# Rotary embedding over 134 MB: two of each partition's sixteen rows of batch 0 stored early by SyncE, and the cosine and sine tables requested from the ScalarE queue

## The chip, the cores and the metric

The kernel runs on one core of a Trainium2 chip. The metric is the device time of one execution in microseconds, lower is better. Each timing is the median of 3 to 11 executions. A profile's "span" is the stretch from the first to the last instruction of the program. The device time is somewhat longer than the span.

## The reference

```python
# x: 8 x 2048 x 16 x 64 float32;  cos, sin: 2048 x 32 float32
x1, x2 = x[..., :32], x[..., 32:]
out1 = x1 * cos - x2 * sin          # cos, sin broadcast over batch and heads
out2 = x1 * sin + x2 * cos
out  = concatenate([out1, out2], axis=-1)      # float32
```

One batch is 8.39 MB in float32. Eight are read and eight are written; the arithmetic is six operations per output pair.

## The kernel before

A row position `s` is split as `s = p*16 + j`, so that each of the 128 partitions holds 16 neighbouring rows. "Two rows" below means two of the 16 in every partition, 1.05 MB in f32. All compute is in f16. The DMAs issued from GpSimd convert f32 to f16 on loading and back on storing; they stand in one ring, in order. Two rows of batch 0 come separately as f32 (`head`) by SyncE, so that something moves before the ring starts, and the last two rows of batch 7 leave the same way.

```python
    J = S // P; NBUF = 5; JA = 2                        # J = 16
    head = const_pool.tile([P, JA, H, D], f32)
    nc.sync.dma_start(out=head..., in_=x0[:, 0:JA, :]...)
    nc.sync.dma_start(out=sin_f, in_=sin.rearrange("(p j) d -> p j d", j=J))
    nc.sync.dma_start(out=cos_f, in_=cos.rearrange("(p j) d -> p j d", j=J))
    # load(b): GpSimd DMA, f32 -> f16 (rows 2..15 for batch 0); store(b, xt): GpSimd DMA, f16 -> f32

    def rotate(xt):
        v = tmp_pool.tile([P, J, H, D], f16)
        # ... broadcasts of sin, -sin and cos over the heads (cut)
        nc.vector.tensor_mul(out=v[:, :, :, 0:Dh], in0=xt[:, :, :, Dh:D], in1=neg_b)
        nc.vector.tensor_mul(out=v[:, :, :, Dh:D], in0=xt[:, :, :, 0:Dh], in1=sin_b)
        nc.vector.tensor_mul(out=xw, in0=xw, in1=cos_b)
        nc.vector.tensor_add(out=xa, in0=xa, in1=v...)

    tiles = [load(b) for b in range(NBUF)]              # five loads at once
    # ScalarE: head -> tile 0, sin_f -> sin_h, -sin_f -> neg_h, cos_f -> cos_h   (cut)
    for b in range(B):
        rotate(tiles[b])
        if b < B - 1:
            store(b, tiles[b])
        if b + NBUF < B:
            tiles.append(load(b + NBUF))                # waits until a buffer's store has landed
    # batch 7 goes out in three parts: 9 rows, 5 rows (ring), 2 rows (ScalarE cast to head, SyncE)   (cut)
```

Of the kernel before, what the change touches and what calls it, by code (L numbers as in the profile page):

```python
# [1 line left out]

# [4 lines left out]


@with_exitstack  # L10
def kernel(
    ctx: ExitStack,
    tc: tile.TileContext,
    x: bass.AP,
    cos: bass.AP,
    sin: bass.AP,
    out: bass.AP,
):
    nc = tc.nc
    f16 = mybir.dt.float16  # L20
    f32 = mybir.dt.float32

    B, S, H, D = x.shape
    Dh = D // 2
    P = nc.NUM_PARTITIONS
    J = S // P
    NBUF = 5

    const_pool = ctx.enter_context(tc.tile_pool(name="rope_const", bufs=1))
    io_pool = ctx.enter_context(tc.tile_pool(name="rope_io", bufs=NBUF))  # L30
    tmp_pool = ctx.enter_context(tc.tile_pool(name="rope_tmp", bufs=1))

    JA = 2
    head = const_pool.tile([P, JA, H, D], f32)
    x0 = x[0].rearrange("(p j) h d -> p j (h d)", j=J)
    nc.sync.dma_start(  # L36
        out=head.rearrange("p j h d -> p (j h d)"),
        in_=x0[:, 0:JA, :].rearrange("p j f -> p (j f)"),
    )
    sin_f = const_pool.tile([P, J, Dh], f32)  # L40
    cos_f = const_pool.tile([P, J, Dh], f32)
    cos_h = const_pool.tile([P, J, Dh], f16)
    sin_h = const_pool.tile([P, J, Dh], f16)
    neg_h = const_pool.tile([P, J, Dh], f16)
    nc.sync.dma_start(out=sin_f, in_=sin.rearrange("(p j) d -> p j d", j=J))  # L45
    nc.sync.dma_start(out=cos_f, in_=cos.rearrange("(p j) d -> p j d", j=J))

    def load(b):
        xt = io_pool.tile([P, J, H, D], f16)
        j0 = JA if b == 0 else 0  # L50
        nc.gpsimd.dma_start(  # L51
            out=xt[:, j0:J, :, :].rearrange("p j h d -> p (j h d)"),
            in_=x[b].rearrange("(p j) h d -> p j (h d)", j=J)[:, j0:J, :].rearrange("p j f -> p (j f)"),
        )
        return xt

    def store(b, xt):
        nc.gpsimd.dma_start(  # L58
            out=out[b].rearrange("(p j) h d -> p (j h d)", j=J), in_=xt
        )  # L60

    def rotate(xt):
        v = tmp_pool.tile([P, J, H, D], f16)
        sin_b = sin_h.unsqueeze(2).to_broadcast([P, J, H, Dh])
        neg_b = neg_h.unsqueeze(2).to_broadcast([P, J, H, Dh])
        cos_b = cos_h.unsqueeze(2).to_broadcast([P, J, 2 * H, Dh])
        nc.vector.tensor_mul(out=v[:, :, :, 0:Dh], in0=xt[:, :, :, Dh:D], in1=neg_b)  # L67
        nc.vector.tensor_mul(out=v[:, :, :, Dh:D], in0=xt[:, :, :, 0:Dh], in1=sin_b)  # L68
        xw = xt.rearrange("p j h (e d) -> p j (h e) d", d=Dh)
        nc.vector.tensor_mul(out=xw, in0=xw, in1=cos_b)  # L70
        xa = xt.rearrange("p j h d -> p (j h d)")
        nc.vector.tensor_add(out=xa, in0=xa, in1=v.rearrange("p j h d -> p (j h d)"))  # L72

    tiles = [load(b) for b in range(NBUF)]
    nc.scalar.copy(  # L75
        out=tiles[0][:, 0:JA, :, :].rearrange("p j h d -> p (j h d)"),
        in_=head.rearrange("p j h d -> p (j h d)"),
    )
    nc.scalar.copy(out=sin_h, in_=sin_f)  # L79
    nc.scalar.mul(out=neg_h, in_=sin_f, mul=-1.0)  # L80
    nc.scalar.copy(out=cos_h, in_=cos_f)  # L81
    def part(b, j0, j1):
        return (
            out[b].rearrange("(p j) h d -> p j (h d)", j=J)[:, j0:j1, :].rearrange("p j f -> p (j f)"),
            tiles[b][:, j0:j1, :, :].rearrange("p j h d -> p (j h d)"),
        )

    for b in range(B):
        rotate(tiles[b])
        if b < B - 1:  # L90
            store(b, tiles[b])
        if b + NBUF < B:
            tiles.append(load(b + NBUF))
    dst, src = part(B - 1, 0, 9)
    gate = nc.gpsimd.dma_start(out=dst, in_=src)  # L95
    dst, src = part(B - 1, 9, J - JA)
    rest = nc.gpsimd.dma_start(out=dst, in_=src)  # L97
    tc.add_manual_dep(
        rest.ins,
        gate.ins.name,  # L100
        mybir.DependencyInfo(mybir.DependencyClass.NoSync, mybir.DependencyReason.DATA),
        reason="order of the ring",
    )
    dst, src = part(B - 1, J - JA, J)
    nc.scalar.copy(out=head.rearrange("p j h d -> p (j h d)"), in_=src)  # L105
    end = nc.sync.dma_start(out=dst, in_=head.rearrange("p j h d -> p (j h d)"))
    tc.add_manual_dep(
        end.ins,
        gate.ins.name,
        mybir.DependencyInfo(mybir.DependencyClass.Sync, mybir.DependencyReason.DATA),  # L110
        reason="the last rows go out behind this part",
    )


# [1 line left out]
_INS = ['x', 'cos', 'sin']  # L116
_OUTS = [((8, 2048, 16, 64), 'float32')]


# [23 lines left out]
```

## Time and profile before

| what | before | where it is read |
|---|---|---|
| device time | 317.36 us, later 317.35 (6 runs) | results |
| span | 315.6 us | page, first line |
| DMA engines busy in the ring's packets | 98.0% of 16 engines | page, part 3 |
| HBM traffic | 134.74 MB, 427 GB/s over the span | page, part 3 |
| VectorE busy | 209.2 us (66%) | page, part 1 |
| batch 0's ring store: issued, turn in the ring, landed | 54.2, about 101, about 121 us | timeline, packet records |
| cos landed | 33.9 us after issue | page, part 6 |

These are lines of the page of the kernel before. The `DMA` line has one digit for each fortieth of the span, and 9 means 90% busy or more. Each queue line has packets, megabytes and the share of 16 engines' span.

```profile
DMA  9899999999999999999999999999999999999998
q0 software_dynamic: 2448, 99.09, 98.0%
q1 hardware_dynamic: 576, 2.62, 2.2%
HBM read 67.63 MB, written 67.11 MB: 427 GB/s over the span
```

There is no idle slice, so there is nothing to hide behind other work. These are lines of the timeline of the kernel before: start in us, duration, engine and line, operation, and in brackets the idle time before it and what ended it.

```profile
1.25 2.79 POOL L51 DMA_DIRECT2D xt<-in_x_dram  x5 [0.80 <-PEq L138]
23.51 4.43 DVE L67 TENSOR_TENSOR v<-xt,neg_h 128x8192 f16<-128x8192 f16 x1 [23.51 <-DMA xt<-in_x_dram]
36.20 8.69 DVE L70 TENSOR_TENSOR xt<-xt,cos_h 128x16384 f16<-128x16384 f16 x1 [3.93 <-ACT cos_h L81]
54.18 0.54 POOL L58 DMA_DIRECT2D out_dram<-xt  x1 [50.14 <-DVE xt L72]
121.83 0.53 POOL L51 DMA_DIRECT2D xt<-in_x_dram  x1 [41.14 <-DMA out_dram<-xt]
...
237.47 4.42 DVE L67 TENSOR_TENSOR v<-xt,neg_h 128x8192 f16<-128x8192 f16 x1 [24.82 <-DMA xt<-in_x_dram]
306.36 0.35 SPq L106 DMA_DIRECT2D out_dram<-head  x1
```

Five loads are issued at the start. VectorE rotates batch 0 from 23.5 us on, with one stall of 3.93 us because cos is late. The store issued at 54.18 us stands behind those five loads in the ring, and the next load (121.83 us) waits for that store.

These are the DMA issues of the kernel before: direction, issuing queue, count, KB each, us from issue to landing.

```profile
head<-in_x_dram SPq DMA_DIRECT2D x1, 1024.0 KB, 4.7
sin_f<-in_sin_dram SPq DMA_DIRECT2D x1, 256.0 KB, 15.2
cos_f<-in_cos_dram SPq DMA_DIRECT2D x1, 256.0 KB, 33.9
```

The trace also holds one record for each DMA packet (start, duration, bytes, queue, not the engine), and a record of 4 bytes where an engine reports a transfer done. A ring transfer has 16 of these 4-byte records. The Trainium skill, "DMA: Bandwidth & Descriptors", section "Why a DMA increments its semaphore by 16 and not by 1", says that with software-generated DMAs all 16 engines post one; the count agrees. So the 16 records of a transfer show when the first, the average and the last engine is through with it. Some of these, put together from the kernel before (the ring's completions in order, us):

```
transfer         first engine   mean     last engine   spread
load 0 (14 rows)     22.64      22.89      23.11        0.47
load 4              101.44     101.62     101.83        0.39
store 0             120.74     120.92     121.13        0.39
load 7              236.68     236.85     237.06        0.39
rows 9-13 of 7      311.55     311.72     311.94        0.39
```

From one full ring packet to the next (65,536 f32 bytes) an engine takes 2.41 us, for loads and stores alike. That is 27.2 GB/s per engine and 435 GB/s for 16.

### The profile page before, as it was taken

How to read it: one execution, taken by the hardware profiler on the slowest of the kernel's cores; microseconds unless marked ns; L12 is line 12 of the kernel's file. 1: busy time of each engine (PE TensorE's matmuls, PEld its weight loads, DVE VectorE, ACT ScalarE, POOL GpSimd, SP SyncE). 2: the span in 40 equal slices, each digit the busy share in tenths (PEclk: the TensorE clock that was granted, in tenths of full speed). 3: DMA queues.
4: the chain of work that ended last, by engine and by line, in shares of the span. 5: the costliest groups of instructions: out<-in, count | busy, mean ns of one | idle time of the engine just before them, and what ended most of it. 6: DMA issues, size and time to landing. Idle time of an engine off the chain costs nothing.

```text
span 315.6 us, 126 instructions
## 1 busy us (share of the span) xinstructions
DVE 209.2 (66%) x32; ACT 6.8 (2%) x6; POOL 9.4 (3%) x21
## 2 busy tenths in 40 slices
DVE  0009599999999999999979999990009994000000
ACT  4010000000000000000000000000000002000000
POOL 3000000000000000010000000100000001000000
DMA  9899999999999999999999999999999999999998
GB/s 278 184 261 207 200 249 216 199 199 249 216 199 266 399 424 507 399 332 233 233 199 199 390 407 399 399 532 266 199 224 507 399 399 498 432 399 399 432 424 341
DMA packets 3024, 101.71 MB, mean 322 GB/s; under 512 B 336, under 2 KB 336, under 8 KB 592
## 3 DMA queue, kind: packets, MB, share of 16 engines
q0 software_dynamic: 2448, 99.09, 98.0%
q1 hardware_dynamic: 576, 2.62, 2.2%
HBM read 67.63 MB, written 67.11 MB: 427 GB/s over the span
## 4 chain that ended last, share of the span: by engine, by line
issue 25%; DMA 23%; DVE 21%; another core or an unknown queue 13%; POOL 1%; ACT 1%; SPq 0%; POOLq 0%; DVEq 0%; ACTq 0%
DMA xt<-in_x_dram 12%; DMA cos_f<-in_cos_dram 11%; DVE xt L70 8%; DVE xt L72 8%; DVE v L68 3%; DVE v L67 1%; ACT head L105 1%; POOL out_dram L58 1%; POOL xt L51 0%; ACT cos_h L81 0%; SPq L45 0%; SPq L36 0%; POOLq L58 0%; DVEq L67 0%
## 5 line engine op out<-in xcount | busy, mean ns | idle before, releaser
L70 DVE TENSOR_TENSOR xt<-xt,cos_h 128x16384 f16<-128x16384 f16 x8 | 69.5, 8692 | 4.2 <-ACT cos_h L81 3.9
L72 DVE TENSOR_TENSOR xt<-xt,v 128x16384 f16<-128x16384 f16 x8 | 69.5, 8692 | 0.3
L67 DVE TENSOR_TENSOR v<-xt,neg_h 128x8192 f16<-128x8192 f16 x8 | 35.4, 4425 | 50.1 <-DMA xt<-in_x_dram 49.9
L68 DVE TENSOR_TENSOR v<-xt,sin_h 128x8192 f16<-128x8192 f16 x8 | 35.3, 4417 | 0.0
L51 POOL DMA_DIRECT2D xt<-in_x_dram x8 | 4.4, 560 | 117.1 <-DMA out_dram<-xt 116.3
L105 ACT CAST head<-xt 128x2048 f32<-128x2048 f16 x1 | 1.9, 1897 | 227.6 <-DVE xt L72 227.6
L58 POOL DMA_DIRECT2D out_dram<-xt x7 | 3.7, 535 | 87.8 <-DVE xt L72 87.8
L95 POOL DMA_DIRECT2D out_dram<-xt x1 | 0.5, 531 | 50.5 <-DVE xt L72 50.5
L75 ACT CAST xt<-head 128x2048 f16<-128x2048 f32 x1 | 1.9, 1898 | 3.4 <-DMA head<-in_x_dram 3.4
L75 ACT ACT_TABLE_LOAD x1 | 1.3, 1283 | 0.7 <-PEq L127 0.7
L81 ACT CAST cos_h<-cos_f 128x512 f16<-128x512 f32 x1 | 0.6, 617 | 18.0 <-DMA cos_f<-in_cos_dram 18.0
L79 ACT CAST sin_h<-sin_f 128x512 f16<-128x512 f32 x1 | 0.6, 617 | 9.1 <-DMA sin_f<-in_sin_dram 9.1
L80 ACT ACTIVATE neg_h<-sin_f 128x512 f16<-128x512 f32 x1 | 0.6, 624 | 0.0
L97 POOL DMA_DIRECT2D out_dram<-xt x1 | 0.5, 531 | 0.0
L127 POOL MEMSET const-float32-0.0<- 128x1 f32 x1 | 0.1, 98 | 0.2 <-issue 0.2
L127 POOL MEMSET const-bfloat16-1.0<- 128x1 bf16 x1 | 0.1, 101 | 0.0
L127 POOL MEMSET const-float32-1.0<- 128x1 f32 x1 | 0.1, 98 | 0.0
L127 POOL MEMSET const-uint8-127<- 128x1 uint8 x1 | 0.1, 98 | 0.0
## 6 DMA issues: line engine op xcount, KB each, us to landing
xt<-in_x_dram POOLq DMA_DIRECT2D x7, 4096.0 KB, 41.1
out_dram<-xt POOLq DMA_DIRECT2D x1, 4608.0 KB, 42.3
xt<-in_x_dram POOLq DMA_DIRECT2D x1, 3584.0 KB, 22.2
out_dram<-xt POOLq DMA_DIRECT2D x1, 2560.0 KB, 47.9
head<-in_x_dram SPq DMA_DIRECT2D x1, 1024.0 KB, 4.7
out_dram<-head SPq DMA_DIRECT2D x1, 1024.0 KB, 8.4
sin_f<-in_sin_dram SPq DMA_DIRECT2D x1, 256.0 KB, 15.2
cos_f<-in_cos_dram SPq DMA_DIRECT2D x1, 256.0 KB, 33.9
```

What stands on the lines that cost most here:

```text
L51: nc.gpsimd.dma_start(out=xt[:, j0:J, :, :].rearrange("p j h d -> p (j h d)"), in_=x[b].rearrange("(p j) h d -> p j (h d)", j=J)[:, j0:J, ...
L58: nc.gpsimd.dma_start(out=out[b].rearrange("(p j) h d -> p (j h d)", j=J), in_=xt)
L67: nc.vector.tensor_mul(out=v[:, :, :, 0:Dh], in0=xt[:, :, :, Dh:D], in1=neg_b)
L68: nc.vector.tensor_mul(out=v[:, :, :, Dh:D], in0=xt[:, :, :, 0:Dh], in1=sin_b)
L70: nc.vector.tensor_mul(out=xw, in0=xw, in1=cos_b)
L72: nc.vector.tensor_add(out=xa, in0=xa, in1=v.rearrange("p j h d -> p (j h d)"))
L75: nc.scalar.copy(out=tiles[0][:, 0:JA, :, :].rearrange("p j h d -> p (j h d)"), in_=head.rearrange("p j h d -> p (j h d)"),)
L79: nc.scalar.copy(out=sin_h, in_=sin_f)
L80: nc.scalar.mul(out=neg_h, in_=sin_f, mul=-1.0)
L81: nc.scalar.copy(out=cos_h, in_=cos_f)
L95: gate = nc.gpsimd.dma_start(out=dst, in_=src)
L105: nc.scalar.copy(out=head.rearrange("p j h d -> p (j h d)"), in_=src)
```

## The change

The intent is to let work on batch 0 begin early: the tables need not queue behind `head`, and two rows go out by SyncE while the ring still loads, which shortens the first ring store.

```diff
-    nc.sync.dma_start(out=sin_f, ...)
-    nc.sync.dma_start(out=cos_f, ...)
+    nc.scalar.dma_start(out=sin_f, ...)
+    nc.scalar.dma_start(out=cos_f, ...)
 ...
     def store(b, xt):
+        j0 = JA if b == 0 else 0            # rows j0..15 only
 ...
-    def rotate(xt):
+    def rotate(xt, j0, j1):                 # the four operations on rows j0..j1-1
 ...
+    rotate(tiles[0], 0, JA)
+    nc.scalar.copy(out=head..., in_=tiles[0][:, 0:JA, :, :]...)
+    nc.sync.dma_start(out=out[0]...[:, 0:JA, :]..., in_=head...)
 ...
-        rotate(tiles[b])
+        rotate(tiles[b], JA if b == 0 else 0, J)
```

More of the change, by code (lines that the diff above doesn't have):

```diff
@@ L44 @@
     neg_h = const_pool.tile([P, J, Dh], f16)
-    nc.sync.dma_start(out=sin_f, in_=sin.rearrange("(p j) d -> p j d", j=J))
-    nc.sync.dma_start(out=cos_f, in_=cos.rearrange("(p j) d -> p j d", j=J))
+    nc.scalar.dma_start(out=sin_f, in_=sin.rearrange("(p j) d -> p j d", j=J))
+    nc.scalar.dma_start(out=cos_f, in_=cos.rearrange("(p j) d -> p j d", j=J))
     def load(b):
@@ L57, in store @@
     def store(b, xt):
+        j0 = JA if b == 0 else 0
         nc.gpsimd.dma_start(
-            out=out[b].rearrange("(p j) h d -> p (j h d)", j=J), in_=xt
+            out=out[b].rearrange("(p j) h d -> p j (h d)", j=J)[:, j0:J, :].rearrange("p j f -> p (j f)"),
+            in_=xt[:, j0:J, :, :].rearrange("p j h d -> p (j h d)"),
         )
-    def rotate(xt):
+    def rotate(xt, j0, j1):
         v = tmp_pool.tile([P, J, H, D], f16)
-        sin_b = sin_h.unsqueeze(2).to_broadcast([P, J, H, Dh])
-        neg_b = neg_h.unsqueeze(2).to_broadcast([P, J, H, Dh])
-        cos_b = cos_h.unsqueeze(2).to_broadcast([P, J, 2 * H, Dh])
-        nc.vector.tensor_mul(out=v[:, :, :, 0:Dh], in0=xt[:, :, :, Dh:D], in1=neg_b)
-        nc.vector.tensor_mul(out=v[:, :, :, Dh:D], in0=xt[:, :, :, 0:Dh], in1=sin_b)
-        xw = xt.rearrange("p j h (e d) -> p j (h e) d", d=Dh)
+        n = j1 - j0
+        js = slice(j0, j1)
+        sin_b = sin_h[:, js, :].unsqueeze(2).to_broadcast([P, n, H, Dh])
+        neg_b = neg_h[:, js, :].unsqueeze(2).to_broadcast([P, n, H, Dh])
+        cos_b = cos_h[:, js, :].unsqueeze(2).to_broadcast([P, n, 2 * H, Dh])
+        nc.vector.tensor_mul(out=v[:, js, :, 0:Dh], in0=xt[:, js, :, Dh:D], in1=neg_b)
+        nc.vector.tensor_mul(out=v[:, js, :, Dh:D], in0=xt[:, js, :, 0:Dh], in1=sin_b)
+        xw = xt[:, js, :, :].rearrange("p j h (e d) -> p j (h e) d", d=Dh)
         nc.vector.tensor_mul(out=xw, in0=xw, in1=cos_b)
-        xa = xt.rearrange("p j h d -> p (j h d)")
-        nc.vector.tensor_add(out=xa, in0=xa, in1=v.rearrange("p j h d -> p (j h d)"))
+        xa = xt[:, js, :, :].rearrange("p j h d -> p (j h d)")
+        nc.vector.tensor_add(out=xa, in0=xa, in1=v[:, js, :, :].rearrange("p j h d -> p (j h d)"))
     tiles = [load(b) for b in range(NBUF)]
@@ L81 @@
     nc.scalar.copy(out=cos_h, in_=cos_f)
+    rotate(tiles[0], 0, JA)
+    nc.scalar.copy(
+        out=head.rearrange("p j h d -> p (j h d)"),
+        in_=tiles[0][:, 0:JA, :, :].rearrange("p j h d -> p (j h d)"),
+    )
+    nc.sync.dma_start(
+        out=out[0].rearrange("(p j) h d -> p j (h d)", j=J)[:, 0:JA, :].rearrange("p j f -> p (j f)"),
+        in_=head.rearrange("p j h d -> p (j h d)"),
+    )
     def part(b, j0, j1):
```

## The prediction

> **What bounds the kernel now.** The 16 DMA engines, almost without a gap. The page's second part shows DMA at 8 or 9 tenths in every slice; its third part gives the gpsimd ring 98.0% of 16 engines' span. HBM moves 67.63 + 67.11 = 134.74 MB at 427 GB/s over the 315.6 us span. The packet records repeat every 2.41 us per engine for 65,536 f32 bytes, in pure-load and pure-store stretches alike: 16 x 65,536 B / 2.41 us = 435 GB/s. The Trainium skill, "DMA: Bandwidth & Descriptors", section "Where 436 GB/s comes from", gives 435 GB/s as the fabric ceiling; this trace agrees. 134.74 MB at that rate is 309.6 us; 1.7 us before the first byte, 1.2 us after the last and some 3 us of small losses make up the span. VectorE is busy 209.2 us (66%) and has slack where it matters: by the timeline it finishes the last batch at 263.7 us, while the ring carries earlier stores until 294.6 us. The first store is issued at 54.2 us but waits behind five loads until about 101 us.
>
> **What the change does.** No byte is removed.
> - Tables on the ScalarE queue: now sin lands 15.2 us and cos 33.9 us after issue, because behind the head load they get one 2 KB packet per long ring packet (2.1 to 2.4 us). The ring's first packet starts at 5.1 us. On its own queue sin alternates with the head's packets (8 per engine, 0.31 us each) and lands near 5 us, cos (estimate) at 16 to 24 us instead of 35.5. VectorE's 3.9 us stall for cos disappears.
> - Batch 0 is rotated in two parts, 2/16 and 14/16: the 26.2 us of work stays, four more instructions cost under 1 us. One more ScalarE cast, 1.9 us.
> - 1.05 MB of batch 0's store leaves the ring and goes out by SyncE at about 24 to 30 us, amid the loads. Its 8 packets per engine each wait behind one ring packet, so it lands about 8 x 2.7 = 22 us after issue. It delays the loads by 2.4 us (8 x 0.31 us); the ring's first store is shorter by the same.
>
> **How much is on the critical path.** None. Batch 0's ring store is issued at about 47 to 52 us, but still queues behind the fifth load. The same page, section "Issuing engines are not separate DMA queues", says all issuers run on the same 16 engines and interleave; the alternating records agree. So the end of that store, which the sixth load awaits (now 121.6 us), stays within 1 us, and the schedule after it is the old one. A few tenths may be won by fewer small packets between ring packets; a few lost by eight interleaved packets and reads mixed with writes.
>
> **Predicted time:** 317.2 us, 8 in 10 between 316.4 and 318.3. Faster by over 2%: 0.01; within 2%: 0.98; slower: 0.01.
>
> **What would show it.** DMA full in all slices, HBM bytes equal; cos landing before 25 us; the early store landing at 45 to 55 us; the fifth load landing about 2.4 us later, but the sixth load issued at 121 to 122 us; the last load landing at 237 us within 1 us; the tail from there unchanged at about 77 us.
>
> **What would make it wrong.** If a hardware-queue write among cast loads costs much more than 0.31 us per packet, the load phase stretches. If reads and writes overlap in an engine, it absorbs the early store and up to 2.4 us are won.

## More of the kernel before

The ring packets just before the first store took 3.19 to 3.38 us instead of 2.43, 0.85 us lost per engine at 98 us. And the engines get out of step by some tenths: 0.47 us when load 0 is done, 0.35 us after load 3, and 0.39 us from load 4 to the end.

## The result, and the profile after

The changed kernel took 318.19 us (median of 6, 317.67 to 319.06) against 317.35 us (6 runs, 317.25 to 317.44): a ratio of 1.0027, interval [1.0013, 1.0041]. Within 2%, that is the same time; within that class it is 0.84 us slower, not faster. Two repeats on two different chips (e1_again and e11_after below) gave 1.0016 [1.0002, 1.0029] and 1.0014 [1.0001, 1.0027].

The page after; `q10` is the ScalarE queue with the tables, `q1` has gained the early store:

```profile
DMA  9999999999999999999999999999999999999997
q0 software_dynamic: 2448, 98.04, 97.1%
q1 hardware_dynamic: 432, 3.15, 2.6%
q10 hardware_dynamic: 288, 0.52, 0.5%
HBM read 67.63 MB, written 67.11 MB: 427 GB/s over the span
```

The same bytes run through the same full engines. The timeline after:

```profile
1.25 2.80 POOL L51 DMA_DIRECT2D xt<-in_x_dram  x5 [0.80 <-PEq L151]
27.10 1.23 DVE L74 TENSOR_TENSOR xt<-xt,cos_h 128x2048 f16<-128x2048 f16 x1 [14.19 <-ACT cos_h L85]
31.60 0.34 SPq L91 DMA_DIRECT2D out_dram<-head  x1
52.93 0.54 POOL L59 DMA_DIRECT2D out_dram<-xt  x1 [48.88 <-DVE xt L76]
122.06 0.54 POOL L51 DMA_DIRECT2D xt<-in_x_dram  x1 [42.35 <-DMA out_dram<-xt]
...
237.43 4.43 DVE L71 TENSOR_TENSOR v<-xt,neg_h 128x8192 f16<-128x8192 f16 x1 [24.76 <-DMA xt<-in_x_dram]
306.34 0.33 SPq L119 DMA_DIRECT2D out_dram<-head  x1
```

The early store is there at 31.60 us. The ring's store is issued 1.25 us earlier (52.93 against 54.18), the load that waits for it 0.23 us later, and the last batch's first operation starts at 237.43 us instead of 237.47. The DMA issues after:

```profile
head<-in_x_dram SPq DMA_DIRECT2D x1, 1024.0 KB, 7.7
sin_f<-in_sin_dram ACTq DMA_DIRECT2D x1, 256.0 KB, 7.9
cos_f<-in_cos_dram ACTq DMA_DIRECT2D x1, 256.0 KB, 25.3
```

The tables do land earlier, cos by 8.6 us, and `head` 3.0 us later: they share the engines now. The profiled execution happens to be the fastest of the six. In it the 4-byte records say:

```
transfer                 first engine   mean     last engine   spread   (before: mean, last)
load 4                      103.45     103.70     104.21        0.76     101.62, 101.83
store 0 (14 rows)           120.34     120.59     121.10        0.76     120.92, 121.13
load 7                      236.27     236.52     237.03        0.76     236.85, 237.06
rows 9-13 of 7              311.14     311.39     311.91        0.76     311.72, 311.94
```

The fifth load is 2.4 us later for the last engine (2.1 us for the average one) and the shorter store after it makes that up, as the bytes say. The average engine is 0.33 us earlier than before. But the engines are twice as far out of step, and the last one, which everything waits for, is not earlier.

### The profile page after: what moved, and what is told of

Same layout as the page of the kernel before. It is cut to its first block, busy times and chain, and to the rows that moved or that the text cites. A ratio compares the mean times of both kernels' runs of the same rounds, so it can differ in the third digit from the quotient of the medians. Undisturbed runs are those within 1.5% of the kernel's fastest.

```text
span 315.6 us, 135 instructions
## 1 busy us (share of the span) xinstructions
DVE 209.7 (66%) x36; ACT 8.6 (3%) x7; POOL 9.4 (3%) x21
## 4 chain that ended last, share of the span: by engine, by line
DVE 23%; DMA 20%; issue 20%; another core or an unknown queue 19%; POOL 1%; ACT 1%; ACTq 0%; POOLq 0%; DVEq 0%
DMA xt<-in_x_dram 12%; DVE xt L76 8%; DVE xt L74 8%; DMA cos_f<-in_cos_dram 8%; DVE v L72 4%; DVE v L71 3%; ACT head L118 1%; POOL out_dram L59 1%; POOL xt L51 0%; ACT cos_h L85 0%; ACTq L45 0%; POOLq L51 0%; POOLq L59 0%; ACTq L118 0%
## 5 line engine op out<-in xcount | busy, mean ns | idle before, releaser
L74 DVE TENSOR_TENSOR xt<-xt,cos_h 128x16384 f16<-128x16384 f16 (+2 forms) x9 | 69.7, 7744 | 14.5 <-ACT cos_h L85 14.2
L76 DVE TENSOR_TENSOR xt<-xt,v 128x16384 f16<-128x16384 f16 (+2 forms) x9 | 69.7, 7743 | 0.3
L71 DVE TENSOR_TENSOR v<-xt,neg_h 128x8192 f16<-128x8192 f16 (+2 forms) x9 | 35.6, 3951 | 39.1 <-DMA xt<-in_x_dram 27.3
L72 DVE TENSOR_TENSOR v<-xt,sin_h 128x8192 f16<-128x8192 f16 (+2 forms) x9 | 35.5, 3944 | 0.0
L118 ACT CAST head<-xt 128x2048 f32<-128x2048 f16 x1 | 1.9, 1897 | 232.1 <-DVE xt L76 232.1
L87 ACT CAST head<-xt 128x2048 f32<-128x2048 f16 x1 | 1.9, 1898 | 2.6 <-DVE xt L76 2.6
```

The lines of the kernel that those rows point to most:

```text
L71: nc.vector.tensor_mul(out=v[:, js, :, 0:Dh], in0=xt[:, js, :, Dh:D], in1=neg_b)
L72: nc.vector.tensor_mul(out=v[:, js, :, Dh:D], in0=xt[:, js, :, 0:Dh], in1=sin_b)
L76: nc.vector.tensor_add(out=xa, in0=xa, in1=v[:, js, :, :].rearrange("p j h d -> p (j h d)"))
L87: nc.scalar.copy(out=head.rearrange("p j h d -> p (j h d)"), in_=tiles[0][:, 0:JA, :, :].rearrange("p j h d -> p (j h d)"),)
L118: nc.scalar.copy(out=head.rearrange("p j h d -> p (j h d)"), in_=src)
```

## The experiments

Twelve runs were made, four to a chip, each beside the kernel before on that chip. Two of them repeat the changed kernel and one repeats e8_nosplit. Three things are read from each: the time, the time minus the span of the same run, and the 4-byte records of its one profile.

Theory A: the early write among the loads costs the time. Theory B: the third queue puts the engines out of step in the first microseconds, and the slowest engine ends the kernel. A third: VectorE's schedule counts.

### Parts of the change alone (first chip; kernel before 317.42 us)

**e1_again**, the changed kernel unaltered:

> The changed kernel unaltered, to see whether its +0.8 us (318.19 against 317.35) and its wide spread (317.67 to 319.06) repeat, and to get a second profile. In the first profile everything after the first gpsimd-ring store is the old schedule to 0.01 us (first store's end to last byte: 193.29 us in both traces), so both theories expect any excess to lie before the end of that store (about 121.1 us). Expected: 318.0 to 318.5 us, and a profile whose span exceeds 315.6 us only by what the first 121 us took longer.

Measured: 317.68 us (317.49 to 318.77), ratio 1.0016 [1.0002, 1.0029]. The median is below the expected band and the spread is as wide as before. In its profile the last engine finished store 0 at 121.44 us and the span was 315.95 us: each is 0.3 us more than before, so the excess lies ahead of that store's end, as expected.

**e2_tables**, only the queue of the tables:

```diff
-    nc.sync.dma_start(out=sin_f, ...)      # and cos_f
+    nc.scalar.dma_start(out=sin_f, ...)    # and cos_f
```

> Only the tables on the ScalarE queue. Theory A (the early SyncE write among the loads costs the time, about 0.1 us per interleaved packet) expects 317.0 to 317.4 us, no slower than before. Theory B (a third queue in the first microseconds puts the 16 engines out of step; spread of the engines' completions was 0.39 us before and 0.76 us after, and the slowest engine ends the kernel) expects 317.8 to 318.3 us and the spread of 0.7 us. Both expect cos to land at 20 to 27 us.

Measured: 317.60 us, ratio 1.0006 [0.9994, 1.0019]; mean span 315.82 us where the kernel before had 315.62. The time falls between the two expected bands. The spread of the engines was 1.03 us, as B has it, but the loss of 0.2 us is too small to be told from nothing by times alone.

**e3_store**, the early store and the split rotation, tables on SyncE (batch 0's ring store is shortened as in the change):

```diff
+    rotate(tiles[0], 0, JA)
+    nc.scalar.copy(out=head..., in_=tiles[0][:, 0:JA]...)
+    nc.sync.dma_start(out=out[0]...[:, 0:JA]..., in_=head...)
```

> Only the early SyncE store (with the split rotation it needs); the tables stay on SyncE. Theory A expects the whole loss here: 317.9 to 318.5 us with a spread as wide as the changed kernel's. Theory B expects 317.2 to 317.5 us. Both expect the store to be issued at about 39 to 41 us (cos lands at 35 us) and to land about 26 us later.

Measured: 317.48 us, ratio 1.0004 [0.999, 1.0017]; mean span 315.46 us, the shortest of the four. Theory A is out: the store costs nothing in the span, and its profile has store 0 done at 120.59 us on average against 120.92. It was issued at 41.01 us and landed about 26 us later, as expected.

**e4_split**, only the split of batch 0's rotation:

```diff
+    rotate(tiles[0], 0, JA)
 ...
-        rotate(tiles[b])
+        rotate(tiles[b], JA if b == 0 else 0, J)
```

> Only the split rotation of batch 0 (2/16 and 14/16), same DMAs as before. VectorE gets four more instructions and batch 0 is ready about 1 us later, but its store waits in the ring until 101 us anyway. Both theories expect 317.3 to 317.5 us, the time before; a third, that VectorE's schedule is on the critical path, expects about +0.5 to +1 us.

Measured: 317.97 us, ratio 1.0017 [1.0005, 1.003]. That is in the band of the third theory, and it was a surprise, since the DMAs are those of the kernel before. Its profiled execution has a span of 315.63 us, that of the kernel before, and yet took 317.68 us. The run lists explain half: in every run of the changed kernel, e3_store and e4_split the time is 2.02 to 2.10 us longer than the span, in every run of the kernel before and of e2_tables 1.73 to 1.82 us. The other half, 0.26 us of mean span (315.88), shows in no profile and stays open.

### What the 0.3 us outside the span is, and what the critical path is made of (second chip; kernel before 318.05 us)

This chip gave the kernel before 0.6 us more than the others, so its results are compared with each other, with one marked exception (e6_no_store).

**e5_pad**, four small VectorE instructions added to the kernel before:

```diff
+    pad = const_pool.tile([P, 64], f16)
+    nc.vector.memset(pad, 1.0)
+    for _ in range(3):
+        nc.vector.tensor_mul(out=pad, in0=pad, in1=pad)
     for b in range(B):
         rotate(tiles[b])
```

> The kernel before plus four small VectorE instructions (a memset and three multiplies of 128x64 on a scratch tile, done before the first rotation); the DMAs and the rotation are unaltered. In the runs so far the time minus the profiled span is 1.73 to 1.82 us in the kernel before and in e2_tables, but 2.02 to 2.10 us in all three variants that split the rotation (changed kernel, e3_store, e4_split). Theory: four more VectorE instructions cost about 0.3 us outside the span. It expects a difference of 2.05 us and a time of 317.6 to 317.8 us. Rival: the split's access patterns or the store cause it; then the difference stays at 1.77 us and the time at 317.4 us.

Measured: time minus span 2.00 to 2.07 us, beside 1.75 to 1.82 us for the kernel before in the same rounds. The additions run while VectorE has nothing to do:

```profile
0.82 0.11 DVE L89 MEMSET pad<- 128x64 f16 x1 [0.82 <-PEq L132]
0.97 0.65 DVE L91 TENSOR_TENSOR pad<-pad 128x64 f16<-128x64 f16 x3
```

So four more VectorE instructions are enough for it; neither the split's access patterns nor the store are needed. Other numbers, and other engines, were not tried. The time itself, 318.12 us, ratio 1.0008 [0.9995, 1.0021], can't be told from the kernel before (and misses the expected band with the chip's slower baseline); the 0.24 us between the means (2.03 and 1.79 us) is seen because span and time of one execution are compared. What the chip does in that time lies outside the profile.

**e6_no_store**, the changed kernel without the early store; two rows of batch 0 are never written, a wrong result:

```diff
-    nc.sync.dma_start(out=out[0]...[:, 0:JA, :]..., in_=head...)
```

> The changed kernel without the early SyncE store: two of sixteen rows of batch 0 are never written (a wrong result on purpose), 1.05 MB less for the DMA engines. If the DMA engines' bytes bound the kernel from end to end, the time falls by 8 packets of 0.30 us per engine, 2.4 us, against the changed kernel: 315.3 to 315.9 us. If that store ran in slack, the time stays at 317.7 to 318.2 us.

Measured: 315.22 us (315.17 to 315.35), the ratio to the kernel before 0.9912 [0.9899, 0.9925].

```profile
HBM read 67.63 MB, written 66.06 MB: 427 GB/s over the span
```

Taking 1.05 MB away takes its time away, 2.4 us by bytes. Its mean span of 313.18 us is 2.6 to 2.9 us below the changed kernel's 315.82 to 316.12 on other chips, so the measured value is a little more than the bytes, and the time fell 0.1 us below the expected band. The changed kernel did not run on this chip; the kernel before had a span of 316.26 us here, 3.1 us more. How much of the excess over 2.4 us is the chip stays open. The store is not in slack. It runs early, but at no less than its full price in bytes.

**e7_late**, VectorE kept busy ahead of batch 0:

```diff
+        if extra:                                   # 3 for batch 0
+            nc.vector.memset(v2, 0.0)
+            for _ in range(extra):
+                nc.vector.tensor_add(out=v2, in0=v2, in1=v2)
```

> The kernel before with VectorE kept busy about 30 us longer (a memset and three additions of 128x16384 on the scratch tile) ahead of batch 0's rotation. Batch 0 is then ready at about 75 to 85 us instead of 54 us, still before its store's turn in the ring at 101 us. Theory (start of batch 0's work is off the critical path): 317.4 to 317.8 us, the higher if the four extra instructions cost 0.3 us outside the span, and the span within 0.3 us of 315.6 us. Rival (earlier work is worth something): 5 us or more are lost.

Measured: 318.44 us, ratio 1.0011 [0.9999, 1.0023]; mean span 316.36 us beside 316.25 for the kernel before. The store was issued at 62.5 us, 8.3 us later than before (less than I meant, because the memset began at 2.5 us), and cost nothing that the four instructions outside the span don't explain:

```profile
62.52 0.54 POOL L58 DMA_DIRECT2D out_dram<-xt  x1 [58.48 <-DVE xt L77]
122.39 0.53 POOL L51 DMA_DIRECT2D xt<-in_x_dram  x1 [33.36 <-DMA out_dram<-xt]
```

The load that waits for the store is issued 0.56 us later than in the profile of the kernel before; that profile is not from these rounds, and this chip gave the kernel before 0.6 us more as well. A start 8.3 us later is off the critical path; the 20 to 30 us meant were not reached. This also speaks against the third theory as the cause of e4_split's longer span, which stays open.

**e8_nosplit**, the candidate: rotation whole, then the two rows by SyncE; tables on SyncE (batch 0's ring store is shortened as in the change):

```diff
         rotate(tiles[b])
+        if b == 0:
+            dst, src = part(0, 0, JA)
+            nc.scalar.copy(out=head..., in_=src)
+            nc.sync.dma_start(out=dst, in_=head...)
```

> A candidate that may beat both: the early SyncE store of two rows of batch 0, but after the whole rotation (no extra VectorE instruction) and with the tables on SyncE. The store is issued at about 56 us and lands near 82 us, before the ring's first store at about 103 us. Theory: 1.77 us outside the span and e3_store's span of 315.3 to 315.7 us, together 317.0 to 317.4 us, 0.1 to 0.3 us below the kernel before. Rival (the store's gain came from its early hour or the table order): 317.4 us or more.

Measured: 317.25 us (one run of six at 318.62), ratio 0.9981 [0.9967, 0.9995]; time minus span 1.74 to 1.82 us. The early cast on ScalarE and the extra SyncE DMA cost nothing outside the span.

### The pause before the first store, and the candidate again (third chip; kernel before 317.46 us)

**e9_order**, batch 0's store put before later loads:

```diff
-    tiles = [load(b) for b in range(NBUF)]
+    tiles = [load(b) for b in range(3)]
 ...
+        if b == 0:
+            tiles.append(load(3))
+            tiles.append(load(4))
```

> The kernel before with batch 0's store put into the ring ahead of the fourth and fifth load (three loads are issued at the start, then store 0, then two loads). In every profile without an early SyncE store the ring packets just before the first ring store take 3.2 to 3.5 us instead of 2.43 us, 0.83 to 1.14 us lost per engine at 96 to 99 us, and never at a later turn from loads to stores. Theory: the first store pays this, wherever it stands. It expects the slow packets at about 60 us now, none at the later turns, and a time within 0.4 us of the kernel before. Rival: it belongs to that hour or to the fifth load; then slow packets stay near 96 to 101 us. If the turn to stores at 60 us left the ring empty, the time would rise by more than 2 us.

Measured: 317.52 us, ratio 1.0000 [0.9987, 1.0012]. The scheduler moved the fourth load up, so four loads, not three, stood before the store, and its turn came at 82 us rather than 60. The four loads and the store after them:

```profile
1.25 2.26 POOL L51 DMA_DIRECT2D xt<-in_x_dram  x4 [0.80 <-PEq L141]
52.11 0.54 POOL L58 DMA_DIRECT2D out_dram<-xt  x1 [48.60 <-DVE xt L72]
```

The late packets moved with it. All 16 packets that started at 78.4 to 79.0 us took 3.18 to 3.95 us, 1.22 us lost per engine, and none later was late. The first store pays, not the hour and not the fifth load. Why it pays, no run shows.

**e10_nosplit_tables**, e8_nosplit with the tables on ScalarE (the edit of e2_tables):

> e8_nosplit with the tables on the ScalarE queue: beside e8_again on the same chip it shows what the table queue alone is worth. Five profiles so far: the first load's mean completion is 23.14 to 23.19 us with the tables on ScalarE and 22.89 to 23.04 us with them on SyncE; the engines' spread is 0.73 to 1.30 us and 0.39 to 0.95 us. Theory: the tables' queue costs 0.1 to 0.4 us of span, so 317.2 to 317.7 us where e8_again has 317.0 to 317.3 us, time minus span at 1.77 us for both. Rival: it costs nothing; then the two agree within 0.1 us.

Measured: 317.92 us, mean span 316.12 us; e12_e8_again beside it has 315.40. So the table queue cost 0.72 us of span here, above the expected 0.1 to 0.4 us. The ranges of the two touch (317.23 to 318.41, 316.92 to 317.75), and the ratio to the kernel before is 1.0013 [0.9999, 1.0027].

**e11_after**, the changed kernel a third time:

> The changed kernel once more, beside e8_again and the kernel before on one chip. Sum of the terms found: +0.29 us outside the span (four more VectorE instructions), about -0.3 us from the shorter pause before the first ring store, +0.1 to +0.5 us from the tables' queue: 0.1 to 0.7 us slower than the kernel before if that chip gives 317.4 us for it, and 0.4 to 0.9 us slower than e8_again. Time minus span 2.05 us.

Measured: 317.75 us, ratio 1.0014 [1.0001, 1.0027]; time minus span 1.96 to 2.09 us. Mean time 317.94 us, 0.76 us above e12_e8_again; mean span 315.90 us, 0.20 us above the kernel before.

**e12_e8_again**, the candidate a second time:

> e8_nosplit repeated: on the first chip it took 317.25 us against 318.05 us for the kernel before. Theory: 317.0 to 317.4 us, 0.1 to 0.8 us below the kernel before, time minus span 1.77 us, ring packets before the first ring store late by 0.1 to 0.6 us. If it isn't below the kernel before here, the gain depends on the chip and is not claimed.

Measured: 317.12 us (316.92 to 317.75), ratio 0.9990 [0.9977, 1.0002]. (The expectation's "first chip" is the one called the second here, where e8_nosplit ran.) It is below the kernel before on both chips, by 0.2% clear of noise on one and 0.1% not quite clear on the other.

### All profiles together

Six columns from the packet records of each profile, in us: load 0 done (mean of the 16 engines); time lost per engine in late ring packets at the first turn to stores; six batches through the ring (store 0 done, by the mean and the last engine, and their spread); and the span minus that last engine's time. (In e9_order the sixth transfer is another, of the same bytes.)

```
                     tables  early   load 0   lost at     store 0   store 0          span -
                     on      store   done     1st store   mean      last     spread   last
before               SyncE   no      22.89    0.85        120.92    121.13    0.39    194.52
e4_split             SyncE   no      23.04    0.99        120.86    121.12    0.47    194.51
e5_pad               SyncE   no      23.03    1.14        120.98    121.57    0.87    194.50
e7_late              SyncE   no      23.00    0.84        121.04    121.70    0.95    194.50
e9_order             SyncE   no      22.90    1.22        120.93    121.22    0.59    194.48
e2_tables            ScalarE no      23.14    1.05        120.83    121.50    1.03    194.50
e6_no_store (-1 MB)  ScalarE none    23.19    0.83        118.26    118.60    0.73    194.52
e3_store             SyncE   yes     22.96    0.60        120.59    120.90    0.59    194.53
e8_nosplit           SyncE   yes     22.96    0.28        120.60    120.85    0.43    194.51
e12_e8_again         SyncE   yes     22.95    0.13        120.37    120.63    0.46    194.52
after                ScalarE yes     23.17    0.36        120.59    121.10    0.76    194.52
e1_again             ScalarE yes     23.16    0.10        120.41    121.44    1.30    194.51
e11_after            ScalarE yes     23.24    0.07        120.38    120.82    0.66    194.51
e10_nosplit_tables   ScalarE yes     23.25    0.07        120.50    121.63    1.39    194.52
```

Three things are to be seen. The last column is constant to 0.05 us in fourteen profiles: once the first six batches are through the slowest engine, the rest of the kernel is a fixed film, and all differences between these kernels arise before 122 us or outside the span. With an early store the late packets at the first ring store cost 0.07 to 0.60 us, without one 0.83 to 1.22 us, and store 0 is done by the mean engine at 120.37 to 120.60 instead of 120.83 to 121.04 us (e6_no_store, which has 1.05 MB less, left aside). And with the tables on ScalarE load 0 is done at 23.14 to 23.25 us on average instead of 22.89 to 23.04, and the spread after store 0 is 0.66 to 1.39 us instead of 0.39 to 0.95. The two large values with the tables on SyncE, 0.87 and 0.95, are from the second chip; on the first and third the groups don't overlap (0.46 to 0.59 and 0.66 to 1.39).

The later load 0 is not a loss. In the changed kernel 226 of the tables' 256 packets have started by 22.7 us, in the kernel before 203, so more of the tables' work stands ahead of the end of load 0 and less behind it. Without an early store the average engine finishes load 3 at 81.16 to 81.22 us with the tables on ScalarE (e2_tables, e6_no_store) and at 81.19 to 81.24 us with them on SyncE (before, e4_split, e5_pad, e7_late). The spread isn't settled in the first microseconds either: when load 0 is done it is 0.42 to 0.91 us with the tables on ScalarE and 0.39 to 1.28 us on SyncE. From load 3 to load 4, just ahead of the first ring store, it grows by 0.17 to 0.35 us in five of the six profiles with the tables on ScalarE (after: 0.55 to 0.76), and by no more than 0.13 us in any with them on SyncE. From there on it stays. So Theory B has the spread right and its hour not shown.

## Why the prediction was right

**The bytes bound the kernel: right.** The same 134.74 MB gave the same span to within 0.2% and 427 GB/s; 1.05 MB less gave about 2.6 to 2.9 us less (e6_no_store). The record-by-record pace of 2.41 us held in every profile.

**No earlier start is on the critical path: right.** Batch 0's ring store was issued at 52.9 us, 0.9 us after the predicted 47 to 52, and it made no difference: the sixth load went out at 122.06 us (121 to 122 predicted). Delaying that store by 8.3 us did no measurable harm (e7_late).

**The early store delays the loads by 2.4 us and the ring's first store gives it back: right.** The last engine finished the fifth load at 104.21 instead of 101.83 us, and store 0 at 121.10 instead of 121.13.

**Landing times: the direction was right, the sizes too small.** Sin was to land near 5 us and landed at 8.6; cos at 16 to 24 us and landed at 26.4, outside the check of 25 us; the early store was issued at 31.6 us instead of 24 to 30 and landed at 58.1 instead of 45 to 55. I counted eight rounds of one ring packet each; 26.5 us from issue to landing at 2.7 us a round are nearly ten. The records show the rest: the first of its packets starts at 35.17 us, 3.6 us after the issue, and behind the last one (55.08 us) the completion record waits for a ring packet too (57.81 us). VectorE's stall for cos did not disappear either, it moved: the two early rows wait 14.2 us for it. None of this is on the critical path, so the time didn't notice.

**The few tenths: the wrong sign.** The prediction put "a few tenths may be won by fewer small packets between ring packets" against "a few lost by eight interleaved packets and reads mixed with writes", and came out 0.16 us below the kernel before. Measured was 0.84 us above, and by the means about 0.5 us above in the two repeats (0.26 and 0.29 us by the medians). That 318.19 us still lies inside the range, 0.11 us under its upper end, is partly luck: the range was wide enough for terms that the sum did not hold. Three terms were found, and only one was in the sum:
- The early store wins rather than loses: about 0.3 us for the mean engine, from the shorter pause at the first ring store. In pairs of mean spans e8_nosplit is 0.60 us and e12_e8_again 0.30 us below the kernel before.
- The tables' own queue loses rather than wins: in the three pairs that differ by it alone the mean span is longer by 0.20 us (e2_tables over the kernel before), 0.36 us (e1_again over e3_store) and 0.72 us (e10_nosplit_tables over e12_e8_again). The average engine is through store 0 no later than with the tables on SyncE; the engines' spread is wider, from store 0 on it stays to 0.01 us in every profile, and the last engine decides. The first two pairs are near their noise; the three agree in sign, and the spread does too. When and why the third queue makes the engines unequal stays open: load 0 doesn't show it, and the records don't name the engine.
- The split adds four VectorE instructions, and those cost 0.25 to 0.3 us that no profile can show, because it lies outside the span (e5_pad).

By the means of the runs, the changed kernel's 318.20 us in the first comparison are 316.12 us of span and 2.08 us outside it; the kernel before, at 317.35 us and 1.77 us outside, has about 315.58 us of span. So 0.3 us of the loss are outside and 0.5 us inside; in the two repeats 0.2 us are inside. The outside part is shown by e5_pad. On the first chip the 0.2 us divide into 0.36 us for the tables' queue (e1_again over e3_store) less 0.16 us for the early store with its split (e3_store under the kernel before). That the 0.5 us are more of the same is argued, not shown. The runs vary by more than that (spans from 315.6 to 317.0 us), and e4_split's 0.26 us has no known cause.

## What to carry to other kernels

When the DMA engines are full from the first to the last slice and one ring is never empty, starting a piece of work earlier buys nothing; only fewer bytes or a smaller loss between packets do. That is what these runs show, for this kernel. Then look at the slowest engine rather than the mean: here the spread that the engines had after the first store (0.39 to 1.39 us) stayed to the end. Compare time minus span between variants, since extra instructions may cost time that no view of the profile shows: four on VectorE cost 0.25 to 0.3 us here. The variant with the early store alone, without the split and without the third queue, was the best of those with right results (317.25 and 317.12 us on two chips), by 0.1 to 0.2%.

## What the Trainium skill lacked or had wrong

- "DMA: Bandwidth & Descriptors", section "SWDGE vs HWDGE vs iDMA", gives a packet as preferably at most 4096 B and the boundary at which an engine changes rings. In this trace a small packet of another queue waits for a whole ring record of 57,344 or 65,536 f32 bytes (for loads, 28,672 or 32,768 bytes in the record, which counts f16), 2.1 to 2.4 us, so cos needed 33.9 us for 256 KB.
- The same page, section "Where 436 GB/s comes from", says without a condition that HBM (about 358 GB/s) binds HBM-to-SBUF transfers. This kernel, on one core, moved 427 GB/s over its whole span and 435 GB/s between packets. The page's own note above that section has the condition, that 358 GB/s is each core's share when both cores of the HBM domain stream; so it is the sentence that misleads, not the page that is wrong.
- The same page, section "Issuing engines are not separate DMA queues", has only sequencer time to be saved by a second issuer. It lacks a cost: with the tables on ScalarE's queue the 16 engines' completions after store 0 spread by 0.66 to 1.39 us instead of 0.39 to 0.95, and the mean span was 0.20 to 0.72 us longer in three pairs, the first two near their noise.
- No page has the pause at the first store among loads: 0.83 to 1.22 us per engine, once, wherever the first ring store stands, and 0.07 to 0.60 us where a small store through another queue went ahead.
- No page has the cost of more VectorE instructions outside the profiled span: four added instructions made the device time minus the span 2.00 to 2.07 us instead of 1.75 to 1.82 us.
